# Queries and keys transposed in fp32 and split on the way out of PSUM, with a planner given new latencies, named buffers and a new order

## The chip, the cores and the metric

The kernel runs on one core of one Trainium2 chip. The core has a matrix engine (TensorE, "PE" in the profile, with its weight loads shown apart as "PEld"), a vector engine (DVE), a scalar engine (ACT), GpSimd (POOL), and a sync engine (SP) that issues the DMA transfers here. The on-chip memory is SBUF, 128 partitions wide; matrix results land in PSUM, which has 8 banks of 128 partitions by 512 fp32 values. The metric is the device time of one execution in microseconds (us); the number of a kernel is the median of its runs.

## The reference, cut to what matters

One inference step of four layers over 128 context tokens and 512 latent tokens, 1024 wide, with 16 query heads and 4 key/value heads of 64 values. Per layer and per group of tokens:

```python
u = rms_norm(h, norm_pre[l]) * (1 + scl) + shift          # scl, shift, gate from SiLU(cond) @ w_mod[l]
p = u @ w_in[l]                                           # 1024 x 2560
q, k, v, z = split(p, [1024, 1280, 1536])
q, k = rms_norm(q, q_norm[l]), rms_norm(k, k_norm[l])     # per head
# layers 0 and 3: rotary positions, all latent keys; layer 1: rotary, a band of +-128 keys and a sink logit;
# layer 2: a 2-D neighbourhood with a bias. Context keys are in every softmax of the latent tokens.
o = softmax(q @ k.T * 64 ** -0.5) @ v
h = h + gate * rms_norm((o * silu(z)) @ w_out[l], norm_post[l])
```

## The kernel before, in words

All data is fp32. A product that matters is made on PE from "fp32r" pieces: a value is rounded to a high part (fp32r) and what is left over is a low part, and PE sums high x high, high x low and low x high. The function `split` (L261, L262) makes the two parts of a 512-wide tile: ACT rounds (L261), DVE or POOL subtracts (L262).

The 640 tokens are five tiles of 128 (tile 0 is the context). Per layer the program does, in this order: `kv_chunk` (keys and values of all five tiles), and then twice, for chunk c = 0 and 1 of eight query heads, `q_chunk` (L597 ff.), the gates `z_block` (L634), the latent attention `lat_pair` four times, and the context attention `ctx_heads`; then `split_og` and `out_phase`, which ends with the normed and transposed input of the next layer.

The scores need the head's 64 values on the partitions. The queries' 128 partitions hold the high part of one head in 64 of them and the low part in the other 64, and the keys hold the same 64 values twice, once as a high tile and once as a low tile (`kst`, with room for two key heads, one buffer, so that chunk 1 builds it anew). Two matmuls of 128 partitions per score (L698, L724, L800) then give (q high + q low) x k high and (q high + q low) x k low.

Before, the parts are made ahead of the transpose. For each of the 40 query tiles (4 layers, 2 chunks, 5 token tiles) and each half of its eight heads, ACT rounds 128x256 values into a tile `hl` (L613), DVE or POOL subtracts (L615), PE transposes four 128x128 blocks with an fp32r identity (L620), and ACT or DVE copies the 128x512 PSUM bank to `q` (L256, a helper's line). For each of the 48 key tiles (4 layers, 2 chunks, 6 tiles, the cached one among them) `k_stack` does the same with the values doubled on the way: round (L544), subtract (L545), four transposes (L553), one copy of 512 columns (L256). The keys of heads 2 and 3 wait for chunk 1 in `kn2` (L591, "kn" in the profile).

The order on every engine is fixed when the program is built. `Sched.op` collects operations with the engines that may do each ("alts"), and `Sched.emit` places them one after another at the time that its own table of durations and latencies gives (`LAT` between engines, `TURN` between kinds of matmul, `SLACK`, and `DISLIKE` for a second choice of engine). `ORDER` shifts the priority of each part of the program ("ks" is `k_stack`, "qt" is `q_chunk`, "mf" the first modulation), and `WINDOW` says how many operations it may run ahead. A tile name is a tag with so many buffers: "B" is four one-bank PSUM buffers, through which every projection, transpose and attention output goes, and "S" is two two-bank ones for scores. The planner takes the buffer that it counts as free first; the tile framework hands out the buffers of a tag in turn.

Of the kernel before, what the change touches and what calls it, by code (L numbers as in the profile page):

```python
# [28 lines left out]
ORDER = {'hn': -470, 'up': -310, 'pv': 20, 'nat': 90, 'tab': -80, 'un': -170, 'bt': -280, 'st': -780, 'out': 230,  # L29
         'z': 90, 'og': -200, 'sc': 180, 'qt': -410, 'no': 180, 'ks': -170, 'mod': 160, 'w': -60}  # L30
MODSHIFT = 100
SSHIFT = -200
WINDOW = 520
PLAT = 270
XLAT = 180
SLACK = {'P': 140, 'V': 0, 'A': 220, 'G': 50, 'D': 80}
DISLIKE = {'Ap': 1060, 'mada': 3020, 'G1': 980, 'mad': 900, 'V': 1260, 'V2': 960, 'G': 780}
# [10 lines left out]
class Buf:  # L48


    def __init__(self, tag, shape, dt):
        self.tag, self.shape, self.dt = tag, shape, dt
        self.ap = None
        self.ops = 0
        self.freed = 0.0
        self.hist = []


class Sched:
# [3 lines left out]
    LAT = {("P", "P"): 0, ("V", "V"): 130, ("A", "A"): 155, ("G", "G"): 110, ("P", "V"): 200, ("P", "A"): 200,  # L63
           ("G", "V"): 80, ("A", "V"): 110, ("V", "A"): 135, ("G", "A"): 150, ("D", "D"): 100, ("V", "P"): 235, ("A", "P"): 228}
# [61 lines left out]
    def emit(self):  # L126
# [8 lines left out]
        slots = {t: [0.0] * c for t, (c, _) in self.tags.items()}  # L135
# [12 lines left out]
        while out < n:  # L148
# [3 lines left out]
            for e, lst in pend.items():  # L152
                cand = None
                for x in lst:
# [12 lines left out]
                    for b in self.ops[i][2]:  # L167
                        if b.ap is None:
                            m = need[b.tag] = need.get(b.tag, 0) + 1
                            s = slots[b.tag]  # L170
                            t = max(t, s[m - 1]) if len(s) >= m else 1e18
# [13 lines left out]
            for b in self.ops[i][2]:  # L185
                if b.ap is None:
                    slots[b.tag].pop(0)
# [7 lines left out]
            done[i] = t + dur + (2000 if e == "D" else 0)  # L195
            where[i] = e
            for b in self.ops[i][2]:
                b.ops -= 1
                b.freed = max(b.freed, done[i])
                if not b.ops:  # L200
                    bisect.insort(slots[b.tag], b.freed + (215 if b.tag in ("S", "B") else 150))
# [7 lines left out]
def build(ctx, tc, a, o):  # L209
# [5 lines left out]
    S = Sched(nc)  # L215

    def sbuf_tag(name, cap):
        S.tag(name, cap, lambda b: sb.tile(b.shape, b.dt, tag=name, name=name, bufs=cap))
# [320 lines left out]
    def k_stack(src, srckey, kst, ct, cap=None):  # L539

        hl = tmp([128, 2, 2, 2, 64], F32R)
        tc_ = [cap, kst] if cap else [kst]
        s = lambda: src()[:, :, None, :].to_broadcast([128, 2, 2, 64])
# [531 lines left out]
```

## Time and profile before

| | us |
|---|---|
| median of 3 runs | 1402.02 |
| lowest, highest | 1398.53, 1402.59 |
| the profiled execution, its own time | 1400.58 |
| its span, first to last instruction | 1398.5 |
| PE busy | 1357.7 |
| DVE busy | 954.7 |
| ACT busy | 758.6 |
| POOL busy | 266.8 |

PE's records are modelled at their ends: a matmul of 128 columns is shown as lasting 0.24 to 0.28 us while the next one starts 0.1 us later, so that PE's work is read from start to start, and a busy share near 100% is not PE at its peak. An idle time shown for PE is what is left after the modelled end of the last matmul.

### The profile page before, as it was taken

Reading aid. Unit: us, or ns where it says so; the run is one execution under the profiler, and the core shown is the slowest. Engines: PE = TensorE matmul, PEld = TensorE weight load, DVE = VectorE, ACT = ScalarE, POOL = GpSimd, SP = SyncE. Lnnn points to the kernel's source line nnn. Section 1 sums busy time; section 2 is a strip of 40 time slices with the busy share of each in tenths; the row PEclk is TensorE's granted clock in tenths of the full one; section 3 lists DMA queues with packets and bytes.
Section 4 is the critical chain, followed back from the end, with each engine's and each line's share of the span. In section 5 each row is a group of like instructions: output and inputs, shape, how many; then the busy total and the mean of one; then the engine's idle time right before and its main releaser. Section 6 shows DMA issues by size and latency. Waiting matters only on the chain.

```text
span 1398.5 us, 25496 instructions
## 1 busy us (share of the span) xinstructions
PE 1357.7 (97%) x9464; PEld 1122.3 (80%) x9464; DVE 954.7 (68%) x2300; ACT 758.6 (54%) x1854; POOL 266.8 (19%) x306
## 2 busy tenths in 40 slices
PE   6999999999999999999999999999999999999998
PEld 3788887888778887887878888888778888778876
DVE  4777667765587786777486676578488876577653
ACT  4556565554355565666354567468345555465641
POOL 1122012010032102201033541441033210021100
PEclk9999999999999999999999999999999999999999
DMA  8522222224532402324542522342633210111032
GB/s 305 175 69 84 61 91 84 69 87 140 181 115 67 147 30 91 125 92 161 161 125 73 157 57 91 98 141 85 196 126 101 91 53 10 61 52 41 31 123 103
DMA packets 73323, 145.11 MB, mean 104 GB/s; under 512 B 8752, under 2 KB 13936, under 8 KB 73200
## 3 DMA queue, kind: packets, MB, share of 16 engines
q1 hardware_dynamic: 73200, 143.50, 31.6%
q8 instruction: 74, 1.21, 0.4%
q14 instruction: 49, 0.40, 0.1%
HBM read 131.90 MB, written 11.57 MB: 103 GB/s over the span
## 4 chain that ended last, share of the span: by engine, by line
PE 83%; DVE 6%; ACT 4%; DMA 3%; issue 3%; POOL 0%; SPq 0%; DVEq 0%; POOLq 0%; ACTq 0%
PE B L497 21%; PE B L634 14%; PE B L780 8%; PE B L773 8%; PE S L901 8%; PE B L901 6%; PE S L698 5%; PE S L724 4%; PE B L383 3%; PE B L620 2%; PE S L497 1%; DVE w L262 1%; DMA raw<-in_w_mod 1%; DMA raw<-in_w_in 1%; PE B L451 1%
## 5 line engine op out<-in xcount | busy, mean ns | idle before, releaser
L307 POOL TENSOR_TENSOR sm<-sm,mhalf 128x1 f32<-128x1 f32 (+2 forms) x100 | 122.1, 1223 | 573.2 <-DVE sm L302 291.5
L497 PE MATMUL B<-w,uB 128*128 128x512 f32 x816 | 207.4, 401 | 0.0
L256 ACT ACTIVATE pt<-B 128x512 f32<-128x512 f32 (+1 forms) x228 | 126.9, 570 | 121.0 <-PE B L773 110.8
L497 PEld LDWEIGHTS B<-w,uB 128*128 128x128 f32 x816 | 149.2, 188 | 31.8 <-DVE uB L262 0.4
L634 PE MATMUL B<-uB,w 128*128 128x384 f32 x768 | 166.0, 348 | 0.6 <-DVE gate L642 0.3
L773 PE MATMUL B<-ident,p 128*128 128x128 f32 x1088 | 159.4, 276 | 3.1 <-ACT pt L256 2.3
L261 ACT ACTIVATE w<-raw 128x512 fp32r<-128x512 f32 x224 | 135.0, 627 | 30.2 <-PE B L901 8.0
L773 PEld LDWEIGHTS B<-ident,p 128*128 128x128 f32 x1088 | 125.1, 141 | 23.7 <-issue 13.6
L262 DVE TENSOR_TENSOR w<-raw,w 128x512 fp32r<-128x512 f32 x193 | 130.5, 700 | 13.0 <-ACT w L261 12.4
L497 PE MATMUL B<-w,uA 128*128 128x512 f32 x528 | 135.1, 403 | 1.1 <-DVE pt L256 0.8
L703 ACT ACTIVATE p<-S,sm 128x640 f32<-128x640 f32 x128 | 101.3, 794 | 59.6 <-DVE sm L701 54.6
L780 PE MATMUL B<-pt,vt 128*64 128x256 f32 (+1 forms) x1152 | 133.0, 376 | 0.0
L634 PEld LDWEIGHTS B<-uB,w 128*128 128x128 f32 x768 | 129.6, 188 | 3.7 <-issue 1.5
L701 DVE TENSOR_REDUCE sm<-S 128x1 f32<-128x640 f32 x128 | 102.7, 819 | 37.7 <-PE S L698 36.8
L634 PE MATMUL B<-uA,w 128*128 128x256 f32 x768 | 117.6, 290 | 0.3 <-DVE modc L394 0.3
L497 PEld LDWEIGHTS B<-w,uA 128*128 128x128 f32 x528 | 96.4, 188 | 24.7 <-DVE w L262 2.1
L780 PEld LDWEIGHTS B<-pt,vt 128*64 128x64 f32 x1152 | 77.5, 137 | 46.0 <-issue 11.4
L634 PEld LDWEIGHTS B<-uA,w 128*128 128x128 f32 x768 | 102.5, 189 | 3.4 <-issue 1.8
L658 DVE TENSOR_SCALAR p<-p,sm 128x640 f32<-128x640 f32 (+2 forms) x197 | 96.9, 506 | 6.6 <-DVE sm L657 0.5
L698 PE MATMUL S<-kst,q 128*128 128x320 f32 x512 | 96.8, 320 | 2.9 <-ACT p L703 2.8
L658 POOL TENSOR_SCALAR p<-p,sm 128x640 f32<-128x640 f32 (+2 forms) x59 | 44.0, 751 | 284.3 <-DVE sm L657 236.4
L737 ACT ACTIVATE p<-p,sm 128x512 f32<-128x512 f32 (+1 forms) x128 | 83.9, 657 | 6.4 <-DVE sm L735 6.3
(148 smaller groups left out, 2216.1 us busy)
## 6 DMA issues: line engine op xcount, KB each, us to landing
raw<-in_w_in SPq DMA_DIRECT2D x160, 256.0 KB
raw<-in_w_mod SPq DMA_DIRECT2D x160, 256.0 KB
raw<-in_w_out SPq DMA_DIRECT2D x64, 256.0 KB
w<-in_w_first SPq DMA_DIRECT2D x16, 512.0 KB
xs<-q SPq DMA_DIRECT2D x15, 512.0 KB
q<-xs SPq DMA_DIRECT2D x15, 512.0 KB
q<-in_x SPq DMA_DIRECT2D x10, 512.0 KB
kst<-gs SPq DMA_DIRECT2D x8, 512.0 KB
```

Of the source, the lines that this page charges most:

```text
L256: alts = {"A": Ap(n, lambda e: e.activation(out(), in_(), AF.Copy)), "V": V(n, lambda e: e.tensor_copy(out(), in_()))}
L261: S.op([As(n, lambda e: e.activation(h(), src(), AF.Copy))], r, w)
L262: f = lambda e: e.tensor_sub(l(), src(), h().bitcast(F32))
L307: S.op([("G", 395 + 157 * n, lambda e: e.tensor_tensor(r.ap, v.ap, mhalf.ap.to_broadcast([128, n]), op=OP.pow), "pow")], r=[v, mhalf], w=[r])
L497: e.matmul(ps(), t.ap[:, s, k, off:off + 128], W[k].ap[:, w], start=k == 0 and i == 0, stop=k == 7 and i == 2)
L634: e.matmul(ps.ap[:, 0:w], W[k].ap[:, wi, 128 * f:128 * f + 128], t.ap[:, s, k, :], start=k == 0 and i == 0, stop=k == 7 and i == 2)
L658: f = lambda e, i=i, p=p, w=w: e.tensor_scalar(p.ap[:, 0:w], p.ap[:, 0:w], rs.ap[:, i:i + 1], 1.0, op0=OP.mult, op1=OP.mult)
L698: e.matmul(ps.ap[:, b, 0:320], Q[t + 1].ap[:, hh], kst.ap[:, g, s, 320 * b:320 * b + 320], start=s == 0, stop=s == 1)
L701: S.op([V(640, lambda e, ps=ps, i=i: e.tensor_reduce(negm.ap[:, i:i + 1], ps.ap[:, :, 0:320], axis=AX.XY, op=OP.max, negate=True))], r=[ps ...
L773: e.transpose(pt.ap[:, c:c + 128], p.ap[:, b:b + 128], ident.ap)
L780: e.matmul(po.ap[64 * x:64 * x + 64, 256 * half + q0:256 * half + q0 + w], vt.ap[:, kt, 64 * g:64 * g + 64], sbt.ap[:, c0:c0 + w], start=f ...
L901: e.matmul(ps(), t.ap[:, s, k, off:off + 128], W[k].ap[:, w], start=k == 0 and i == 0, stop=k == 7 and i == 2)
```

## The change

The values are transposed first, in fp32, and split afterwards on the way out of PSUM.

Queries: per tile, PE transposes four 128x128 blocks of two heads each, in fp32 (L618 of the new file), into one PSUM bank. For each parity x of the head, ACT rounds the 64 partitions that hold those heads into `q` (64 x 512 values, L625), and DVE subtracts the rounded values from PSUM into the other 64 partitions of the same head (L626). The sum over the 128 partitions is the same; scores of a head wait for its parity and no longer for its half.

Keys: the doubling is a copy of its own (`kd`, ACT L595 or DVE L596; `kn2` is kept doubled, L592, and the cached keys are loaded twice by DMA). PE transposes two 128x128 blocks in fp32 (L550), ACT rounds 128x256 from PSUM into `kst` (L554), DVE subtracts into `kst` (L555).

Planner: other latencies, a landing time of 4 us for a DMA in place of 2, a `WINDOW` of 257 in place of 520, new weights, and a buffer of a tag is now a tag of its own ("B0" to "B3"), so that the buffer that the planner took is the one used.

```diff
-ORDER = {'hn': -470, 'up': -310, 'pv': 20, 'nat': 90, 'tab': -80, 'un': -170, 'bt': -280, 'st': -780, 'out': 230,
...
+ORDER = {'mf': -51, 'tab': 230, 'kv': 673, 'ks': -1156, 'nat': 29, 'hn': -564, 'mod': 211, 'w': -2, 'qt': 6,
...
-WINDOW = 520
...
+WINDOW = 257
 PLAT = 270
+LAND = 4000
...
-        slots = {t: [0.0] * c for t, (c, _) in self.tags.items()}
+        slots = {t: [(0.0, k) for k in range(c)] for t, (c, _) in self.tags.items()}
...
-                    slots[b.tag].pop(0)
+                    b.slot = slots[b.tag].pop(0)[1]
                     b.ap = self.tags[b.tag][1](b)
...
-        S.tag(name, cap, lambda b: pp.tile(b.shape, b.dt, tag=name, name=name, bufs=cap))
+        S.tag(name, cap, lambda b: pp.tile(b.shape, b.dt, tag="%s%d" % (name, b.slot), name=name, bufs=1))
...
-        hl = tmp([128, 2, 2, 2, 64], F32R)
...
-        S.op([As(256, lambda e: e.activation(hl.ap[:, 0], s(), AF.Copy))], r=[srckey], w=[(hl, 0)], touch=tc_)
-        f = lambda e: e.tensor_sub(hl.ap[:, 1], s(), hl.ap[:, 0].bitcast(F32))
-        S.op([G(256, f), VL(256, f)], r=[srckey, (hl, 0)], w=[(hl, 1)], touch=tc_)
...
+            for g in range(2):
+                e.transpose(ps.ap[:, 128 * g:128 * g + 128], src()[:, g].rearrange("p a d -> p (a d)"), ident.ap)
+        S.op([P(218, tr, "T")], r=[srckey, ident], w=[ps], touch=tc_)
+        v = lambda: ps.ap[:, 0:256].rearrange("p (g c) -> p g c", g=2)
+        d = lambda i: kst.ap[:, :, i, 128 * COL[ct]:128 * COL[ct] + 128]
+        S.op([As(256, lambda e: e.activation(d(0), v(), AF.Copy))], r=[ps], w=[(kst, ct)])
+        S.op([V(256, lambda e: e.tensor_sub(d(1), v(), d(0).bitcast(F32)))], r=[ps, (kst, ct)], w=[(kst, ct)])
...
+            pt = S.buf("B", [128, 512])
+
+            def tr(e, pt=pt, qn=qn):
+                for pr in range(4):
+                    e.transpose(pt.ap[:, 128 * pr:128 * pr + 128], qn.ap[:, 2 * pr:2 * pr + 2].rearrange("p h d -> p (h d)"),
+                                ident.ap)
+            S.op([P(436, tr, "T")], r=[qn, ident], w=[pt], touch=[cap])
+            for x in range(2):
+                hi, lo = (slice(0, 64), slice(64, 128))[::1 - 2 * x]
+                d = lambda rows, x=x, q=q: q.ap.rearrange("p (r x) t -> p x r t", x=2)[rows, x]
+                v = lambda hi=hi, pt=pt: pt.ap[hi].rearrange("p (r t) -> p r t", r=4)
+                S.op([As(512, lambda e, d=d, v=v, hi=hi: e.activation(d(hi), v(), AF.Copy))], r=[pt], w=[(q, x)], touch=[cap])
+                S.op([V(512, lambda e, d=d, v=v, hi=hi, lo=lo: e.tensor_sub(d(lo), v(), d(hi).bitcast(F32)))], r=[pt, (q, x)],
+                     w=[(q, x)], touch=[cap])
```

What the planner makes of it is seen in the instructions of each engine in program order. The rows give the line, the operation, the tiles out<-in, the shape written, and how many in a row.

PE in the projection of layer 0's first query chunk, before (L497 is the projection, L620 the query transposes, L698 scores):

```order
L497 MATMUL B<-w,uB 128x512 x21
L620 MATMUL B<-identr,tmp 128x128 x4
L497 MATMUL B<-w,uB 128x512 x3
L620 MATMUL B<-identr,tmp 128x128 x4
L497 MATMUL B<-w,uB 128x512 x18
L620 MATMUL B<-identr,tmp 128x128 x4
```

and now (L501 is the projection, L618 the query transposes, L387 a modulation):

```order
L618 MATMUL B<-ident,tmp 128x128 x4
L501 MATMUL B<-w,uA 128x512 x3
L501 MATMUL B<-w,uB 128x512 x30
L618 MATMUL B<-ident,tmp 128x128 x4
L501 MATMUL B<-w,uB 128x512 x18
L387 MATMUL B<-raw,cpad 32x128 x16
```

Where a query tile had two groups of four transposes, with projection matmuls between, it has one group of four.

PE at the change from chunk 0 to chunk 1 in layer 3, before (L800 context scores, L773 and L826 transposes of probabilities, L553 key transposes, L780 attention outputs, L634 gates):

```order
L634 MATMUL B<-uA,w 128x256 x9
L800 MATMUL S<-kst,q 128x128 x8
L773 MATMUL B<-ident,p 128x128 x8
L553 MATMUL B<-identr,tmp 128x128 x8
L780 MATMUL B<-pt,vt 64x256 x10
L553 MATMUL B<-identr,tmp 128x128 x16
L634 MATMUL B<-uB,w 128x384 x9
L826 MATMUL B<-ident,p 128x128 x4
```

and now (L804 context scores, L550 key transposes, which read `kn2` itself, L830 transposes of probabilities, L501 the projection of chunk 1):

```order
L638 MATMUL B<-uB,w 128x384 x24
L830 MATMUL B<-ident,p 128x128 x4
L804 MATMUL S<-kst,q 128x128 x8
L501 MATMUL B<-w,uA 128x512 x3
L550 MATMUL B<-ident,kn_11649 128x128 x6
L501 MATMUL B<-w,uA 128x512 x3
L550 MATMUL B<-ident,kn_11649 128x128 x2
L501 MATMUL B<-w,uA 128x512 x3
L550 MATMUL B<-ident,kn_11649 128x128 x4
```

The 24 key transposes became 12, and projection matmuls stand between their groups.

SP, the first transfers of the program, before (L340 and L344 load the first modulation weights, `cnd` is the conditioning vector, `q` the input rows):

```order
L280 DMA cnd<-in_cond 128x16
L329 DMA bcol<-in_vec 128x40
L296 DMA sink<-in_sink 128x16
L340 DMA w<-in_w_first 128x1024 x2
L969 DMA q<-in_x 128x1024
L340 DMA w<-in_w_first 128x1024 x2
```

and now:

```order
L344 DMA w<-in_w_first 128x1024 x4
L284 DMA cnd<-in_cond 128x16
L333 DMA bcol<-in_vec 128x40
L300 DMA sink<-in_sink 128x16
L973 DMA q<-in_x 128x1024
```

The conditioning vector now stands behind four transfers of 512 KB, and the first input rows behind the same four.

## Rows read from the trace of the kernel before

**Rows 1.** The page, busy time of each engine with its share of the span and its instructions, and TensorE's granted clock in 40 slices of the span (tenths of full speed).

```profile
PE 1357.7 (97%) x9464; PEld 1122.3 (80%) x9464; DVE 954.7 (68%) x2300; ACT 758.6 (54%) x1854; POOL 266.8 (19%) x306
...
PEclk9999999999999999999999999999999999999999
```

**Rows 2.** The page, the chain of work that ended last, shares of the span by engine.

```profile
PE 83%; DVE 6%; ACT 4%; DMA 3%; issue 3%; POOL 0%; SPq 0%; DVEq 0%; POOLq 0%; ACTq 0%
```

**Rows 3.** Busy time by stretch: the stretch and its length in us, busy us and instructions of each engine, granted clock, share of the DMA engines, GB/s. 400 to 457 and 1045 to 1110 are the starts of layers 1 and 3 (keys, values and queries).

```profile
0.00:50.00 50.00, 37.94 (x240) 24.15 (x240) 28.82 (x87) 21.20 (x53) 7.08 (x14) 1.00 0.85 302
...
400.00:457.00 57.00, 56.48 (x277) 45.57 (x277) 44.72 (x106) 30.05 (x68) 15.85 (x13) 1.00 0.24 78
...
1045.00:1110.00 65.00, 64.90 (x340) 53.95 (x339) 52.83 (x120) 36.80 (x82) 22.82 (x17) 1.00 0.24 80
1110.00:1200.00 90.00, 85.50 (x712) 71.42 (x711) 57.93 (x123) 52.38 (x126) 6.38 (x8) 0.98 0.14 47
...
1334.00:1398.50 64.50, 57.81 (x257) 45.56 (x255) 27.50 (x49) 16.62 (x40) 2.77 (x5) 0.97 0.32 111
```

**Rows 4.** PE in time order at the start of layer 1: start, length, engine, line, operation, out<-in, shapes, how many in a row.

```profile
405.29 4.39 PE L497 MATMUL B<-w,uB 128*128 128x512 f32 x18
...
409.51 0.46 PE L553 MATMUL B<-identr,tmp 128*128 128x128 f32 x4
...
409.81 0.93 PE L497 MATMUL B<-w,uB 128*128 128x512 f32 x3
...
410.58 0.46 PE L553 MATMUL B<-identr,tmp 128*128 128x128 f32 x4
...
410.88 3.74 PE L497 MATMUL B<-w,uB 128*128 128x512 f32 x15
```

**Rows 5.** PE in time order in layer 0, chunk 1, the same columns.

```profile
241.59 0.63 PE L634 MATMUL B<-uA,w 128*128 128x256 f32 x3
...
242.05 0.60 PE L773 MATMUL B<-ident,p 128*128 128x128 f32 x4
...
242.41 0.78 PE L634 MATMUL B<-uB,w 128*128 128x384 f32 x3
...
245.50 0.81 PE L620 MATMUL B<-identr,tmp 128*128 128x128 f32 x8
```

**Rows 6.** All engines in time order at the change of chunks in layer 3, the same columns as rows 4; in brackets the idle time before the piece and what ended it.

```profile
1189.13 1.07 PE L773 MATMUL B<-ident,p 128*128 128x128 f32 x8
...
1189.26 1.96 ACT L544 ACTIVATE tmp<-kn 128x256 fp32r<-128x256 f32 x6
...
1190.01 2.09 DVE L545 TENSOR_TENSOR tmp<-kn,tmp 128x256 fp32r<-128x256 f32 x6
...
1191.76 0.53 PE L553 MATMUL B<-identr,tmp 128*128 128x128 f32 x4 [1.56 <-ACT pt L256]
...
1193.05 3.76 PE L780 MATMUL B<-pt,vt 128*64 128x256 f32 x20
...
1196.74 1.05 PE L553 MATMUL B<-identr,tmp 128*128 128x128 f32 x8
1197.50 2.32 ACT L256 ACTIVATE kst<-B 128x512 fp32r<-128x512 f32 x4 [2.58 <-PE B L553]
...
1198.15 1.02 PE L553 MATMUL B<-identr,tmp 128*128 128x128 f32 x8 [0.36 <-ACT kst L256]
...
1199.38 1.85 PE L634 MATMUL B<-uB,w 128*128 128x384 f32 x9 [0.21 <-ACT kst L256]
```

**Rows 7.** What PE waited for: us in total, times, longest.

```profile
PE B L773 <- ACT pt L256: 2.3, 5, 0.7
...
PE B L553 <- ACT pt L256: 1.9, 2, 1.6
```

**Rows 8.** Groups by line, the copies, roundings and subtractions that stand nearest to the old and the new ones: busy us, mean ns of one | idle us before them, and what ended it.

```profile
L256 ACT ACTIVATE q<-B 128x512 fp32r<-128x512 f32 x78 | 45.0, 595 | 31.9 <-PE B L620 31.6
...
L615 DVE TENSOR_TENSOR tmp<-tmp 128x256 fp32r<-128x256 f32 x78 | 32.2, 435 | 12.9 <-ACT tmp L613 12.7
...
L613 ACT ACTIVATE tmp<-tmp 128x256 fp32r<-128x256 f32 x80 | 29.5, 410 | 68.1 <-DVE tmp L534 41.9 <-DVE tmp L528 26.0
...
L945 DVE TENSOR_TENSOR tmp<-B,kst 128x512 f32<-128x512 f32 x20 | 13.7, 687 | 21.0 <-ACT tmp L943 21.0
```

**Rows 9.** Groups by line, work that DVE and POOL share, and DVE's work on a query tile; columns as in rows 8.

```profile
L262 DVE TENSOR_TENSOR w<-raw,w 128x512 fp32r<-128x512 f32 x193 | 130.5, 700 | 13.0 <-ACT w L261 12.4
...
L658 DVE TENSOR_SCALAR p<-p,sm 128x640 f32<-128x640 f32 (+2 forms) x197 | 96.9, 506 | 6.6 <-DVE sm L657 0.5
...
L658 POOL TENSOR_SCALAR p<-p,sm 128x640 f32<-128x640 f32 (+2 forms) x59 | 44.0, 751 | 284.3 <-DVE sm L657 236.4 <-DVE sm L654 14.3 <-DMA raw<-in_w_in 13.3
L262 POOL TENSOR_TENSOR w<-raw,w 128x512 fp32r<-128x512 f32 x31 | 43.6, 1409 | 138.4 <-ACT w L261 135.8 <-issue 2.6
...
L510 DVE TENSOR_TENSOR tmp<-B,sm 128x512 f32<-128x512 f32 (+1 forms) x56 | 34.2, 611 | 44.4 <-POOL sm L307 44.3
...
L528 DVE TENSOR_TENSOR tmp<-tmp 128x512 f32<-128x512 f32 (+1 forms) x36 | 21.8, 606 | 0.3
```

**Rows 10.** DVE in time order at the start of layer 1, columns as in rows 4.

```profile
412.66 0.42 DVE L521 TENSOR_TENSOR tmp<-tmp,tab 128x256 f32<-128x256 f32 x1
...
413.00 0.42 DVE L523 TENSOR_TENSOR tmp<-tmp,tab 128x256 f32<-128x256 f32 x1
```

More of the change, by code (lines that the diff above doesn't have):

```diff
@@ L53, in __init__ @@
         self.ap = None
+        self.slot = 0
         self.ops = 0
@@ L170, in emit @@
                             s = slots[b.tag]
-                            t = max(t, s[m - 1]) if len(s) >= m else 1e18
+                            t = max(t, s[m - 1][0]) if len(s) >= m else 1e18
                     if t < 1e17:
@@ L194, in emit @@
                 last = x[2][3]
-            done[i] = t + dur + (2000 if e == "D" else 0)
+            done[i] = t + dur + (LAND if e == "D" else 0)
             where[i] = e
@@ L200, in emit @@
                 if not b.ops:
-                    bisect.insort(slots[b.tag], b.freed + (215 if b.tag in ("S", "B") else 150))
+                    bisect.insort(slots[b.tag], (b.freed + (170 if b.tag in ("S", "B") else 190), b.slot))
             out += 1
@@ L590, in kv_chunk @@
                 S.op([D(128, lambda e: e.dma_start(o["nv"][0, l].rearrange("t h d -> t (h d)"), vt.ap[:, VC, :]))], r=[(vt, VC)])
-            S.op([As(128, lambda e, kn=kn, ct=ct: e.activation(kn2.ap[:, ct], kn.ap[:, 2:4], AF.Copy))], r=[kn], w=[(kn2, ct)],
+            two = lambda k0, kn=kn: kn.ap[:, k0:k0 + 2, None, :].to_broadcast([128, 2, 2, 64])
+            S.op([As(256, lambda e, two=two, ct=ct: e.activation(kn2.ap[:, ct], two(2), AF.Copy))], r=[kn], w=[(kn2, ct)],
                  touch=[cap])
-            k_stack(lambda kn=kn: kn.ap[:, 0:2], kn, kst, ct, cap)
+            kd = tmp([128, 2, 2, 64])
+            S.op([As(256, lambda e, two=two, kd=kd: e.activation(kd.ap, two(0), AF.Copy)),
+                  V2(256, lambda e, two=two, kd=kd: e.tensor_copy(kd.ap, two(0)))], r=[kn], w=[kd], touch=[cap, kst])
+            k_stack(lambda kd=kd: kd.ap, kd, kst, ct, cap)
         return kst, vt, kn2
@@ L699, in mm @@
                                      start=s == 0, stop=s == 1)
-                S.op([P(588, mm)], r=[(Q[t + 1], hh // 4)] + [(kst, x) for x in range(5)], w=[ps], seq="s")
+                S.op([P(588, mm)], r=[(Q[t + 1], hh % 2)] + [(kst, x) for x in range(5)], w=[ps], seq="s")
                 S.op([V(640, lambda e, ps=ps, i=i: e.tensor_reduce(negm.ap[:, i:i + 1], ps.ap[:, :, 0:320], axis=AX.XY, op=OP.max,
@@ L724, in mm @@
                             e.matmul(ps.ap[:, i, o:o + n], Q[t + 1].ap[:, hh], v(s), start=s == 0, stop=s == 1)
-                S.op([P(w * 0.88 + 14, mm)], r=[(Q[t + 1], hh // 4)] + [(kst, x) for x in BAND[t]], w=[(ps, i)], seq="s")
+                S.op([P(w * 0.88 + 14, mm)], r=[(Q[t + 1], hh % 2)] + [(kst, x) for x in BAND[t]], w=[(ps, i)], seq="s")
                 bb, bap = bias[t]
```

52 lines of the change are left out of this document (17 added, 35 removed).

## Prediction

> **What bounds the kernel now.** I read the page's busy times first. PE is busy for 1357.7 of 1398.5 us at the full granted clock in every slice; DVE has 954.7 us and ACT 758.6 [rows 1]. The chain that ended last agrees: 83% of it is PE, 6% DVE, 4% ACT, 3% DMA [rows 2]. So a us of work taken from PE is a us of time, unless PE waits for data at that place, and work on DVE and ACT counts only where it makes PE wait. Then the stretches, for where PE stands idle: 40.8 us in all (1398.5 - 1357.7), of which 12.1 us lie in the first 50 us, where DMA runs at 302 GB/s, 6.7 us in the last 64.5, and 4.5 us between 1110 and 1200 [rows 3]. Some 17.5 us are left for all the rest. Last, the timeline, from start to start, for what a transpose costs PE.
>
> **PE's transposes.** Eighteen projection matmuls of 512 columns take 4.22 us to the next start, 0.234 each, so that a matmul of 256 columns is half, 0.117 [rows 4]. A group of four fp32r transposes takes 0.30 us from its first start to the next projection matmul (409.51 to 409.81, 410.58 to 410.88). The second of these begins 0.77 us after three projection matmuls that need 0.70, so 0.07 us late; with that the group costs 0.37 us [rows 4]. The fp32 transpose is there already, for the probabilities. Four of them begin 0.46 us after three matmuls that need 0.35, which is 0.11 late, and hold PE for 0.36 us, together 0.47 [rows 5]; eight in a row last 1.07 us against 0.60 for four, 0.12 each [rows 5, 6].
>
> A query tile has two groups of four before, 0.74 us, and one now, 0.47. Over 40 tiles that is 40 x 0.27 = 10.8 us. A key tile has one group of four before, 0.37, and two transposes now, 0.47 - 2 x 0.12 = 0.23; 48 x 0.14 = 6.7 us. Together -17.5 us, of which I take -17, since some groups stand back to back before and pay the 0.07 once (eight last 0.81 us against 0.46 for four [rows 4, 5]). If the late starts belong to the neighbours and not to fp32r, the group costs 0.30 and the saving is 40 x 0.13 + 48 x 0.07 = 8.6 us. If they belong to fp32r alone and the fp32 group costs 0.36, it is 40 x 0.38 + 48 x 0.25 = 27 us. I stay at 17, which charges both kinds alike.
>
> **The change of chunks.** In layer 3 the keys of chunk 1 are rounded by ACT (1.96 us for six), subtracted by DVE (2.09 us), transposed in 24 pieces and copied by ACT (four copies in 2.32 us), and the key buffer is single. PE starts its first group at 1191.76 after 1.56 us idle and reaches the gates at 1199.38, 7.62 us later; its work in between is 24 x 0.09 for the transposes (0.81 / 8 is 0.10 with the tail [rows 5]) and 20 x 0.117 for the attention output, 4.5 us [rows 6]. So PE loses 1.56 + 3.1 = 4.7 us there. Now the doubled keys lie ready in `kn2`, the first step is the transpose itself, and the list of PE shows three projection matmuls between the groups. What is late next are ACT's rounding and DVE's subtraction into `kst`, and their first readers are scores that come after the projection, so the projection hides them. I take -5 us for all four layers: layer 3 nearly whole, and little elsewhere. Bounds: nothing, if the same idle time returns ahead of the first transposes, and -9 if the other layers hold as much again.
>
> **Buffers and order.** PE waits for a "B" bank that ACT or DVE has still to empty: 2.3 us for the probabilities' transposes, 1.9 us for the keys' [rows 7], and smaller ones. A buffer used out of turn ends some of these, and the new order can end others. Apart from the first 50 us, the last 64.5 and the 4.7 us above, about 17 us of idle time are there to be had. I take -5, near what the bank waits sum to. It cannot be below -17; on the other side, a poor order could add as much as the start shows, +12.
>
> **The start.** `cnd`, which the first matmul needs, stands behind four transfers of 524 KB now and stood ahead of all. At 302 GB/s [rows 3] four take 6.9 us, and the first matmul needs two of them anyway, so it comes up to 3.5 us later. As the same bytes must land by about 50 us, most of it is made up again. I take +1, between -2 and +3.5.
>
> **ACT and DVE.** A query tile cost ACT 2 x (0.410 + 0.595) = 2.01 us and now two roundings of 64 x 512 from PSUM, which I price as the copy of the same 512 columns, 2 x 0.595 = 1.19 [rows 8]. It cost DVE 2 x 0.435 = 0.87, and now 2 x 0.687 = 1.37, by the nearest subtraction-like row with a PSUM input and 512 columns [rows 8]: half the lanes stand idle, so the values cost nearly twice. That is +0.50 x 40 = 20 us on DVE. The planner also gives DVE 47 of the 59 scalings that POOL did (47 x 0.506 = 24 us) and 19 of its 31 weight subtractions (19 x 0.70 = 13 us) [rows 9], and takes the copies of transposed probabilities from it (72 of 76 go to ACT), which about repays this. Price zero, hidden by PE; the price without that cover is the last rival.
>
> A subtraction that reads 64 partitions and writes the other 64 has no row before. Two DVE instructions of the usual kind overlap: one starts at 412.66, lasts 0.42 us, and the next starts at 413.00, 0.08 us before its end [rows 10]. [...]
>
> **The sum.** -17 - 5 - 5 + 1 = -26 us. The profiled execution took 1400.58 us, of which 2.1 us lie outside its span, and 1400.6 - 26 = 1374.6. The median of the runs is 1402.0, 1.4 us above the profiled one, and 0.1% is less than I can tell apart. I predict 1374 us, with 1366 to 1382 for this case by itself.
>
> **The rivals.** *Only the transposes.* The order and the buffers bring nothing and the idle time moves elsewhere: 1400.6 - 17 + 1 = 1384.6, and up to 1394 with the lower bound of the transposes. For it: the planner's table of durations is not the chip, and 17 us of idle time over 1300 us is already little. Against: the 4.7 us in layer 3 hang on a chain that the change takes apart.
>
> *The idle time goes.* The named buffers end the bank waits and the order most other idle time: -17 - 8 - 13 + 0, 1362.6 us. For it: PE is at 98% outside the first 50 us, so its waits are short and many, the kind that a better order ends. Against: many of them are latencies between engines that no order removes where nothing else is ready.
>
> *The saving is hidden.* PE waits for the last query tile anyway, and its shorter transposes only lengthen that wait: 1400 us. For it: ACT's rounding waited 41.9 + 26.0 us for the query tiles' last DVE step [rows 8], so that chain is late. Against: PE itself has only 0.5 us idle in 400 to 457 and 0.1 in 1045 to 1110 [rows 3], where these chains lie.
>
> *DVE becomes late, and the kernel slower.* The place is the projection of queries at the start of a layer. DVE is at 52.8 of 65 us from 1045 to 1110, 81% [rows 3]. A query tile costs DVE one reduction and one scaling of about 0.61, three rope steps of 0.606 and the subtractions 0.87, 3.9 us, and 8 x 0.70 / 5 = 1.1 us of weight subtractions go with it [rows 8, 9], 5.0 in all; PE needs 24 x 0.234 = 5.6 us for the tile [rows 4]. With 0.50 more and POOL's share of the weights, DVE stands at 5.5 to 6, and it decides from 5.6 on. At 6.3 us, with other work between, each of 40 tiles loses 0.7, 28 us: 1400.6 - 17 + 1 + 28 = 1413 us. [...] Against: PE has key transposes, modulations and gates to put in between.
>
> **How the numbers follow.** The forecast has 0.50, only the transposes 0.22, the idle time goes 0.16, the saving is hidden 0.05, DVE late 0.07. A difference under 0.3% (4.2 us) I call no change, about what a measurement of this kernel can tell. Faster: 0.50 + 0.22 + 0.16 = 0.88; same 0.05; slower 0.07. The range runs from 1357, just under the case in which the idle time goes, to 1394, the worst of only the transposes; what is outside is the two last cases and the tails, under 0.2.
>
> **What would show it.** 160 transposes on L618 and 96 on L550, with groups of four at 0.36 to 0.47 us from start to start. At the change of chunks in layer 3 no wait of PE ahead of the key transposes. L625 near 0.6 us, L626 near 0.7. PE's idle time between the first 50 us and the last 64 at about 12 us. PE at its first matmul some 3 us later than before. I am wrong if PE's idle time grows in 400 to 457 or 1045 to 1110 behind L626 or L555 (DVE late), or if PE's transposes do not get cheaper by the count.

## The result, and the profile after

| | before | after |
|---|---|---|
| median of the runs, us | 1400.28 (4 runs) | 1367.61 (4 runs) |
| lowest, highest | 1398.34, 1402.59 | 1366.54, 1369.06 |
| profiled execution, own time and span | 1400.58, 1398.5 | 1366.54, 1364.8 |

The ratio is 0.9767, interval 0.9745 to 0.9788: 32.7 us less, where 26 were forecast. The time lies in the forecast's own range and the direction is right. The runs below show that its parts were not: with the new planner the data path brought half of what was forecast for it, and the planner four times as much.

The page of after, busy times and the chain by engine; they answer to [rows 1, 2].

```profile
PE 1331.3 (98%) x9208; PEld 1097.1 (80%) x9208; DVE 971.9 (71%) x2298; ACT 753.5 (55%) x1823; POOL 212.9 (16%) x231
...
PE 80%; DVE 13%; issue 3%; ACT 2%; POOL 1%; DMA 1%; SPq 0%; DVEq 0%; POOLq 0%; ACTq 0%
```

Of the 33.7 us by which the span fell (1398.5 - 1364.8), 26.4 are PE's busy time (1357.7 - 1331.3) and 7.3 its idle time (40.8 - 33.5). DVE is 17.2 us busier and POOL 53.9 us less.

Busy time by stretch, columns as in [rows 3]: the start, the start of layer 1, the middle, the change of chunks in layer 3, the end.

```profile
0.00:50.00 50.00, 37.57 (x267) 24.43 (x268) 31.11 (x97) 23.01 (x58) 6.72 (x13) 1.00 0.88 314
...
400.00:457.00 57.00, 55.74 (x327) 45.34 (x326) 45.82 (x102) 25.18 (x50) 15.62 (x11) 1.00 0.31 100
50.00:1300.00 1250.00, 1235.74 (x8683) 1026.66 (x8682) 912.63 (x2153) 712.48 (x1723) 203.46 (x213) 1.00 0.31 98
1110.00:1200.00 90.00, 89.44 (x655) 75.24 (x654) 58.81 (x118) 53.58 (x127) 4.76 (x4) 1.00 0.14 47
1300.00:1364.80 64.80, 58.04 (x262) 46.02 (x260) 28.15 (x51) 18.02 (x43) 2.76 (x5) 0.96 0.34 118
```

Idle time of PE (a stretch less PE's busy time in it): 12.4 us at the start (12.1 before), 14.3 in the middle (22.0 before, which is 40.8 - 12.1 - 6.7), 6.8 at the end (6.7). All of the gain in idle time lies in the middle. In 1110 to 1200 it is 0.6 us, against 4.5 [rows 3].

The timeline of the start of layer 1, columns as in [rows 4, 6]: one query tile.

```profile
425.09 2.35 PE L501 MATMUL B<-w,uA 128*128 128x512 f32 x9
...
427.28 0.60 PE L618 MATMUL B<-ident,tmp 128*128 128x128 f32 x4
...
427.63 1.65 PE L501 MATMUL B<-w,uA 128*128 128x512 f32 x6
427.91 1.20 ACT L625 ACTIVATE q<-B 64x512 fp32r<-64x512 f32 x2 [4.05 <-PE B L618]
...
429.14 1.39 DVE L626 TENSOR_TENSOR q<-B,q 64x512 fp32r<-64x512 f32 x2 [2.59 <-ACT q L625]
```

Nine projection matmuls need 9 x 0.234 = 2.11 us, the transposes begin 2.19 us after the first of them, 0.08 late, and hold PE for 0.35: 0.43 for the group, read as the prediction reads it. The single starts in the trace show that this lateness does not stand ahead of the transposes. It is in the second matmul behind a group, which comes 0.30 us (fp32r, before) or 0.32 us (fp32, now) after the first in place of 0.23. The bank that they fill is free again at 430.53, when DVE's second subtraction ends, 2.9 us after PE has left it. Remember this span; the experiments come back to it.

Over all 40 query tiles the bank is held for a median 2.92 us behind the transposes; before, one copy emptied it, in a median 0.80 us (80 groups). The four steps that empty it now go one after another: in 37 of the 40 tiles the first subtraction starts only when the second rounding has ended, 0.64 us or more after the first rounding, which is the only one that it reads. That wait is part of the 2.9 us; no run takes it away.

The change of chunks in layer 3, the same columns, in place of [rows 6].

```profile
1176.62 0.92 PE L501 MATMUL B<-w,uA 128*128 128x512 f32 x3
...
1177.37 0.81 PE L550 MATMUL B<-ident,kn 128*128 128x128 f32 x6
1177.79 0.94 ACT L554 ACTIVATE kst<-B 128x256 fp32r<-128x256 f32 x3 [1.22 <-PE B L550]
...
1177.94 0.96 PE L501 MATMUL B<-w,uA 128*128 128x512 f32 x3
1178.20 1.08 DVE L555 TENSOR_TENSOR kst<-B,kst 128x256 fp32r<-128x256 f32 x3 [0.19 <-ACT kst L554]
...
1178.74 0.38 PE L550 MATMUL B<-ident,kn 128*128 128x128 f32 x2
...
1178.88 0.95 PE L501 MATMUL B<-w,uA 128*128 128x512 f32 x3
```

No PE row has a bracket, so the trace shows no wait of PE here: the projection matmuls fill the time in which ACT and DVE empty the banks.

Groups by line, columns as in [rows 8].

```profile
L626 DVE TENSOR_TENSOR q<-B,q 64x512 fp32r<-64x512 f32 x80 | 55.1, 689 | 34.9 <-ACT q L625 33.8
...
L625 ACT ACTIVATE q<-B 64x512 fp32r<-64x512 f32 x80 | 47.4, 593 | 54.4 <-PE B L618 53.7
...
L618 PE MATMUL B<-ident,tmp 128*128 128x128 f32 x160 | 24.8, 277 | 6.1 <-DVE tmp L532 5.1 <-DVE tmp L538 0.6 <-DVE modc L398 0.3
...
L550 PE MATMUL B<-ident,tmp 128*128 128x128 f32 x48 | 9.1, 273 | 0.0
...
L550 PE MATMUL B<-ident,kn 128*128 128x128 f32 x48 | 7.2, 273 | 0.0
```

The counts are those forecast: 160 transposes on L618 and 96 on L550.

PE's waits: us in total, times, longest.

```profile
PE B L350 <- DMA raw<-in_w_in: 10.9, 1, 10.9
PE B L618 <- DVE tmp L532: 5.1, 10, 0.7
...
PE B L777 <- ACT pt L260: 0.8, 3, 0.5
```

The largest wait behind the start is now that for the last rope step of a query tile (L532), ten times half a microsecond; the wait of the probabilities' transposes for a bank fell from 2.3 us [rows 7] to 0.8, and that of the key transposes is gone.

### The profile page after: what moved, and what is told of

The parts are those of the page before. It is cut to its first block, busy times and chain, and to the rows that moved or that the text cites. A ratio compares the mean times of both kernels' runs of the same rounds, so it can differ in the third digit from the quotient of the medians.

```text
span 1364.8 us, 24827 instructions
## 1 busy us (share of the span) xinstructions
PE 1331.3 (98%) x9208; PEld 1097.1 (80%) x9208; DVE 971.9 (71%) x2298; ACT 753.5 (55%) x1823; POOL 212.9 (16%) x231
## 4 chain that ended last, share of the span: by engine, by line
PE 80%; DVE 13%; issue 3%; ACT 2%; POOL 1%; DMA 1%; SPq 0%; DVEq 0%; POOLq 0%; ACTq 0%
PE B L501 16%; PE B L638 13%; PE B L777 9%; PE B L784 9%; PE S L905 8%; PE B L905 6%; PE S L702 5%; PE S L728 4%; PE B L387 2%; DVE q L626 2%; DVE tmp L467 1%; POOL sm L311 1%; DVE w L266 1%; PE S L501 1%; PE B L618 1%
## 5 line engine op out<-in xcount | busy, mean ns | idle before, releaser
L311 POOL TENSOR_TENSOR sm<-sm,mhalf 128x1 f32<-128x1 f32 (+2 forms) x100 | 130.3, 1305 | 667.6 <-DVE sm L306 352.5
L260 ACT ACTIVATE pt<-B 128x512 f32<-128x512 f32 (+1 forms) x300 | 161.2, 575 | 101.8 <-PE B L777 91.7
L501 PE MATMUL B<-w,uB 128*128 128x512 f32 x816 | 201.3, 399 | 0.0
L501 PEld LDWEIGHTS B<-w,uB 128*128 128x128 f32 x816 | 150.0, 188 | 33.4 <-issue 0.2
L777 PE MATMUL B<-ident,p 128*128 128x128 f32 x1088 | 155.1, 277 | 2.1 <-ACT pt L260 0.8
L266 DVE TENSOR_TENSOR w<-raw,w 128x512 fp32r<-128x512 f32 x212 | 141.7, 698 | 5.7 <-ACT w L265 5.2
L777 PEld LDWEIGHTS B<-ident,p 128*128 128x128 f32 x1088 | 122.5, 140 | 24.0 <-issue 8.8
L501 PE MATMUL B<-w,uA 128*128 128x512 f32 x528 | 136.9, 403 | 0.8 <-DVE tmp L467 0.7
L265 ACT ACTIVATE w<-raw 128x512 fp32r<-128x512 f32 x224 | 131.7, 626 | 6.6 <-PE B L638 2.8
L662 DVE TENSOR_SCALAR p<-p,sm 128x640 f32<-128x640 f32 (+2 forms) x244 | 123.7, 519 | 6.8
L638 PE MATMUL B<-uA,w 128*128 128x256 f32 x768 | 114.7, 286 | 0.1
L501 PEld LDWEIGHTS B<-w,uA 128*128 128x128 f32 x528 | 95.1, 188 | 23.0 <-issue 2.6
L702 PE MATMUL S<-kst,q 128*128 128x320 f32 x512 | 100.5, 324 | 1.1 <-ACT p L707 0.8
L510 ACT ACTIVATE tmp<-B 128x512 f32<-128x512 f32 (+1 forms) x56 | 30.1, 537 | 106.0 <-PE B L501 82.6
```

The source lines that it names most:

```text
L260: alts = {"A": Ap(n, lambda e: e.activation(out(), in_(), AF.Copy)), "V": V(n, lambda e: e.tensor_copy(out(), in_()))}
L265: S.op([As(n, lambda e: e.activation(h(), src(), AF.Copy))], r, w)
L266: f = lambda e: e.tensor_sub(l(), src(), h().bitcast(F32))
L311: S.op([("G", 395 + 157 * n, lambda e: e.tensor_tensor(r.ap, v.ap, mhalf.ap.to_broadcast([128, n]), op=OP.pow), "pow")], r=[v, mhalf], w=[r])
L501: e.matmul(ps(), t.ap[:, s, k, off:off + 128], W[k].ap[:, w], start=k == 0 and i == 0, stop=k == 7 and i == 2)
L638: e.matmul(ps.ap[:, 0:w], W[k].ap[:, wi, 128 * f:128 * f + 128], t.ap[:, s, k, :], start=k == 0 and i == 0, stop=k == 7 and i == 2)
```

## The experiments

The change has three parts: the data path (transpose, then split), the buffers by name, and the planner's numbers. Two theories stood against each other. By the first the terms add: each part brings its own share whatever the others are. By the second the data path alone gives little or loses, because the bank is held while ACT and DVE split, and only an order made for that brings the gain out. Every kernel below computes the whole reference. The number given first is the median, the one in brackets the ratio to the kernel before, run on the same chip, with its interval; that kernel's medians there were 1398.7 to 1399.8 us.

### The data path alone: slower

```diff
 # before, with k_stack, kv_chunk, q_chunk of after
 WINDOW = 520
+LAND = 2000
 # ORDER, LAT, SLACK, DISLIKE and the buffers in turn as before
```

> The transposes in fp32 and the split from PSUM alone; latencies, weights, window and buffers in turn as before. Theory A (the parts add: some 18 us of PE work from the transposes and some 15 us of waits from the planner): 1382 us, 1377 to 1387, PE idle about as before, 41 us. Theory B (the gain is the search's, and PE's saved work turns into waits without it): 1393 us or more, PE idle 50 us or more.

Measured: 1410.83 us (1.0097, 1.0071 to 1.0122), 12 us slower than before. What PE waited for:

```profile
PE B L616 <- DVE tmp L530: 4.4, 8, 0.8
PE B L636 <- DVE q L624: 3.9, 3, 1.3
PE B L548 <- DVE kst L553: 3.7, 6, 1.6
...
PE B L548 <- DMA tmp<-in_cache_k: 2.7, 4, 1.2
```

The second and third lines are new waits: gates (L636) and key transposes (L548) wait for a bank which DVE's subtractions from PSUM (L624, L553) still read. The last is new too: the cached keys are transposed as they land, and four times PE waits for their transfer. Neither before nor after has such a wait. The timeline of PE at the change of chunks in layer 2:

```profile
863.67 0.38 PE L548 MATMUL B<-ident,kn 128*128 128x128 f32 x2
865.63 0.44 PE L548 MATMUL B<-ident,kn 128*128 128x128 f32 x2 [1.58 <-DVE kst L553]
867.00 0.60 PE L548 MATMUL B<-ident,kn 128*128 128x128 f32 x2 [0.93 <-DVE kst L553]
868.25 0.66 PE L548 MATMUL B<-ident,kn 128*128 128x128 f32 x2 [0.65 <-DVE tmp L512]
868.71 1.06 PE L775 MATMUL B<-ident,p 128*128 128x128 f32 x4
```

And the stretches there, columns as in [rows 3]:

```profile
860.00:866.00 6.00, 4.42 (x22) 3.23 (x21) 2.72 (x7) 2.93 (x12) 0.27 (x1) 1.00 0.31 106
866.00:872.00 6.00, 3.94 (x16) 2.69 (x15) 2.88 (x6) 2.74 (x6) 1.38 (x1) 0.59 0.00 0
872.00:878.00 6.00, 5.11 (x24) 3.10 (x25) 1.72 (x4) 1.28 (x3) 0.00 (x0) 0.55 0.00 0
```

With the old order the key transposes follow each other with nothing between, and PE does eight of them in 5 us. The first two waits are for a bank that L553 reads; the third is for one that holds a projection of queries, until its norm has read it (L512). Behind that, the granted clock is lower: 0.59 and 0.55 of full speed in the two stretches from 866 to 878 us, against 1.00 ahead of them. The mean is 0.57 over 12 us, by which I estimate a loss of up to 12 x 0.43 = 5 us of PE's work. In all PE is idle for 55.2 us of 1407.8, 14.4 more than before. Its busy time fell by only 5.1 us (1357.7 to 1352.6), although it has 256 matmuls less to do.

### The planner and the names on the old data path

```diff
 # before, with ORDER, shifts, WINDOW, LAND, LAT, SLACK, DISLIKE and the named buffers of after
```

> The planner's part alone (latencies, landing time, weights, window, named buffers) on the old way of splitting ahead of the transpose. Theory A: 1386 us, 1381 to 1392, PE idle about 30 us. Theory B: 1378 us or less. Theory C (weights searched for one program are worth nothing on another): 1397 us or more.

Measured: 1379.00 us (0.9858, 0.9838 to 0.9877). The new numbers bring 20 us without any change of the data path. Together with the run before: -20 and +12 would add to -8; the change brings -31 to -33. The terms do not add, so the second theory stands in its main point, though the time is a microsecond above the 1378 that it allowed.

This run also prices the data path where it is used. It and after have the same planner and the same names, and their tiles lie alike (the step of their matmuls, explained below, is 232.2 ns in both). Its page:

```profile
PE 1348.1 (98%) x9464; PEld 1119.5 (81%) x9464; DVE 941.5 (68%) x2286; ACT 789.2 (57%) x1935; POOL 215.6 (16%) x239
```

Against after (1331.3) the new path takes 16.8 us from PE's busy time. PE's idle time is 4.5 us longer with it (33.5 against 1377.1 - 1348.1 = 29.0), and the median falls by 10.6 us (1379.0 to 1368.4). So the same path is worth -11 us with the new planner and +12 with the old one.

And it shows where the wait at the change of chunks in layer 3 went, for here the keys are still split ahead of the transpose:

```profile
1190.60 1.14 PE L557 MATMUL B<-identr,tmp 128*128 128x128 f32 x12
1191.58 0.94 PE L501 MATMUL B<-w,uA 128*128 128x512 f32 x3
1192.35 1.14 PE L557 MATMUL B<-identr,tmp 128*128 128x128 f32 x12
```

All 24 old key transposes (L557) stand between projection matmuls, and no row has a bracket: the new order alone ends that wait.

### The names alone

```diff
-        S.tag(name, cap, lambda b: sb.tile(b.shape, b.dt, tag=name, name=name, bufs=cap))
+        S.tag(name, cap, lambda b: sb.tile(b.shape, b.dt, tag="%s%d" % (name, b.slot), name=name, bufs=1))
 # the same for PSUM; all else as before
```

> Named buffers alone on the kernel before. Theory A, as in the prediction: -5 us, 1395 us, PE's waits for a bank on L773, L553 and L620 (5.6 us before) mostly gone. Rival: the buffers in turn were the planner's choice nearly always, 1400 us, the same waits.

Measured: 1393.42 us (0.9962, 0.9949 to 0.9974), 5.4 us less, which is the size forecast. But not for the reason given. Its waits for banks are those of [rows 7] to the digit:

```profile
PE B L774 <- ACT pt L257: 2.3, 5, 0.7
PE B L554 <- ACT pt L257: 1.9, 2, 1.6
```

No wait for a bank went, so the gain came from elsewhere. The trace has one thing more, at the change of chunks in layer 3. After the same wait of 1.55 us the 20 attention outputs take

```profile
1189.15 2.38 PE L781 MATMUL B<-pt,vt 128*64 128x256 f32 x20
```

where before they took 3.76 [rows 6]. The granted clock is 1.00 here; in the profiled execution of before it stood at 0.50 from 1194 to 1197 us, columns as in [rows 3]:

```profile
1194.00:1197.00 3.00, 3.00 (x16) 1.46 (x13) 0.87 (x2) 0.92 (x6) 0.00 (x0) 0.50 0.00 0
```

### After, with the buffers in turn

```diff
-        S.tag(name, cap, lambda b: sb.tile(b.shape, b.dt, tag="%s%d" % (name, b.slot), name=name, bufs=1))
+        S.tag(name, cap, lambda b: sb.tile(b.shape, b.dt, tag=name, name=name, bufs=cap))
 # the same for PSUM; all else as after
```

> The changed kernel with its buffers handed out in turn again, the order of the instructions unchanged. Theory A: 1373 us, 1370 to 1377, waits for banks come back. Rival: 1367 to 1369 us, names are worth nothing.

Measured: 1363.05 us (0.9749, 0.973 to 0.9768): 5 us faster than after, where 5 slower were expected, or no difference. The order of the instructions is the same in both. What differs is where the tiles lie in SBUF, and it shows in how long the same matmuls take: the last 96 of the program (w_out, 512 columns) in the chain of waits, columns start, length, piece, of after

```profile
1330.12 22.33 PE B L905 x96
```

and of this kernel

```profile
1326.23 21.99 PE B L905 x96
```

They wait for nothing inside, and take 3.5 ns less each (0.34 us / 96). No run had changed the place alone yet; the next one does.

### Moving the tiles by 32 bytes

```diff
 # the kernel with the buffers in turn
-    keps = persist("keps", [128, 1])
+    keps = persist("keps", [128, 9])
```

One constant is 32 bytes longer, so that what is allocated behind it, `uA` and `uB` among it, begins 32 bytes later. Nothing else changes.

> The changed kernel with its buffers in turn, every instruction the same and in the same order, but one constant made 32 bytes longer, so that the inputs' tiles uA and uB and all behind them lie 32 bytes further in SBUF, while the weights' tiles stay. Theory H (names and turns differ by where the tiles lie: the 2400 projection matmuls of 512 columns started 229.3 ns apart there and 232 to 234 ns apart in the other kernels, whose tiles lie otherwise): steps of 232 to 234 ns, 6 to 10 us more than with the buffers in turn, 1369 to 1373 us. Rival (what differs are the waits for buffers): 1362 to 1365 us, steps of 229 ns.

Measured: 1369.34 us (0.9798, 0.9775 to 0.9822), 6.3 us slower than without the 32 bytes. The same piece of the chain:

```profile
1331.53 22.41 PE B L905 x96
```

With 32 bytes moved and nothing else, the time thus grew by 6.3 us. From the start times of the 2400 projection and output matmuls of 512 columns, the mean step from one to the next, by where the operands in the weights tile `w` and the input tile `u` begin in SBUF (bytes in the partition, remainder by 64; the addresses are those of the built programs, the steps are from the traces):

| kernel | w, u | step, ns |
|---|---|---|
| before; the data path alone, and with 'pv' (below) | 0, 32 | 234.0 |
| after, mean 232.2 | mixed: 1080 of 2400 at 32, 0, 720 at 32, 32 | by place 231.1 to 233.0 |
| after, buffers in turn; the data path with the new ORDER (below) | 32, 32 | 229.3 |
| the same, 32 bytes moved | 32, 0 | 233.1 |

The remainder by 64 alone does not tell the step: at 32, 32 it is 229.3 ns with the buffers in turn and 231.1 in after. By the steps the 32 bytes would cost 2400 x 3.8 ns = 9.1 us, of which 6.3 came out in the time; presumably some of these matmuls do not bound it. From before to after the mean falls by some 1.8 ns, and up to 2400 x 1.8 = 4.3 us of the result may be placement, which nobody set. Of the names' 5.4 us this may be a part as well (step 234.0 to 232.8, up to 2400 x 1.2 = 2.9 us). Both are estimates from the steps. At the start that kernel is 2.4 us ahead of before at the same matmul (at 46 us) and keeps 1.4 of it from 52 us on. The rest of the 5.4 is not told apart.

### After with the old weights

```diff
 # after, with ORDER, shifts, WINDOW, LAND, SLACK, DISLIKE of before
 # (LAT and the named buffers stay new)
```

> The changed kernel with the new latencies and named buffers, but the old weights, window, slack and landing time. Theory D (the weights found by the search carry the gain: without them PE waits behind the split of the keys at the change of chunks): 1395 to 1412 us, idle time of PE ahead of the key transposes in layers 2 and 3 as in the run of the data path alone. Rival (the latencies, and the names, carry it): 1380 us or less.

Measured: 1403.74 us (1.0028, 1.001 to 1.0045). The weights carry the gain: 35 us lie between this kernel and after (1368.39 beside it), and by the step of its matmuls (232.8 against 232.2 ns) I put up to 2400 x 0.6 = 1.4 of them down to placement. The place of its waits is not quite the one expected: the key transposes wait 1.3 us in all for a bank that the subtraction reads, against 3.7 in the data path alone, but scores wait 5.3 us for the queries' subtraction itself (L625 of this kernel), and the query transposes 5.2 us for the rope step.

### Only the queries new, old planner

```diff
 # before, with the query half of the data path (L613 to L626); keys as before
```

> Only the queries on the new way, keys on the old one, planner as before. Theory D (what cost the data path alone its 12 us is the key split, whose banks are held through ACT and DVE): 1386 to 1392 us, near the 10.8 us that the query transposes take from PE. Rival (the query split costs as much, by DVE's longer subtraction): 1398 us or more.

Measured: 1404.49 us (1.0036, 1.0021 to 1.005), 5 us slower than before. The idea that the keys alone cost the 12 us fell: the queries cost 5 of them, and the keys add about 7. The wait for the rope step and the one for the queries' bank are as with both halves:

```profile
PE B L616 <- DVE tmp L530: 5.0, 9, 0.8
PE B L636 <- DVE q L624: 3.8, 3, 1.3
```

### The weights rounded, and after again

```diff
-ORDER = {'mf': -51, 'tab': 230, 'kv': 673, 'ks': -1156, 'nat': 29, 'hn': -564, ...
+ORDER = {'mf': -50, 'tab': 230, 'kv': 670, 'ks': -1160, 'nat': 30, 'hn': -560, ...
-WINDOW = 257
+WINDOW = 260
```

> The changed kernel with each weight rounded to tens and a window of 260 in place of 257, a neighbour of the order found. If the search found one lucky order, a neighbour loses most of the planner's share: 1376 us or more. If the weights stand for a rule (keys early, the softmax early), the neighbour is within 4 us: 1363 to 1372.

> The changed kernel again, beside the others on one chip: 1365 to 1370 us. If it lies at 1363 here, the buffers in turn gained nothing over the names in the earlier run.

Measured: 1369.98 us (0.9788, 0.9756 to 0.9819) and 1368.39 us (0.9772, 0.9745 to 0.98). The gain does not hang on the exact numbers: it outlives the rounding of the weights. The step is a small one, though. No weight moves by more than 5, and PE has the same instruction at 8314 of its 9208 places, so a farther neighbour might still lose the gain.

### The data path with the new ORDER alone, and with one entry of it

```diff
 # the data path alone, with the whole ORDER of after
```

> The data path with the planner as before and only the table of the parts' weights from the change: latencies, window, slack, dislikes, shifts and landing time as before, buffers in turn. Theory J (that table is what turns the loss of the data path into the gain): 1375 to 1387 us. Rival (it needs the other numbers with it): 1395 us or more.

Measured: 1384.74 us (0.9908, 0.9882 to 0.9934), 26 us less than the data path alone. But this kernel is no clean comparison, for its tiles came to lie at 32, 32, where the step is 229.3 ns, and those of the data path alone at 0, 32. By the steps that is 2400 x 4.7 = 11 us, and some 8 if as much of it comes out as with the 32 bytes (6.3 / 9.1). So the priorities themselves have about 15 to 18 of the 26, an estimate from the steps; they were not run at the old placement.

```diff
 # the data path alone
-ORDER = {'hn': -470, 'up': -310, 'pv': 20, ...
+ORDER = {'hn': -470, 'up': -310, 'pv': -1242, ...
```

> As the data path alone, with one weight changed: the part that transposes probabilities and makes the attention outputs gets -1242 in place of 20, so that it goes as soon as it can and projections are left to stand between the waits. Theory K (this one weight is half of it): 1390 to 1400 us. Rival: 1406 us or more, since at the change of chunks in layers 0, 2 and 3 no projection stands between the key transposes with it.

Measured: 1400.11 us (1.0005, 0.9988 to 1.0022), 11 us less than the data path alone, at the edge of what was expected. This comparison is clean: the step is 234.0 in both. 'pv', the attention outputs and the transposes of probabilities before them, is less than half of the 26 but most of the 15 to 18 that belong to the order. It brings the path level with before, no more.

### The fastest order with the start of before

```diff
 # after, buffers in turn; the tiles kept at the same remainders by padding
+    S.shift = -3000    # cnd is loaded ahead of the weights
```

> The changed kernel with its buffers in turn and the conditioning vector loaded first, the tiles placed as with the buffers in turn modulo 128 bytes. Theory I (PE's first matmul waits for the vector, 10.5 us in place of 6.5, and the start is made up only in part): first matmul at 6 to 7 us, 1359 to 1361 us. Rival (the start is bound by the bytes of the transfers): 1362 to 1364 us.

Measured: 1362.98 us (0.9756, 0.9733 to 0.9779), no different from the 1363.05 without it. PE's first wait:

```profile
PE B L352 <- DMA w<-in_w_first: 5.5, 1, 5.5
```

The first matmul comes 5.0 us earlier (10.5 there), and by 77 us PE has done 63.55 us of work against 63.52. So the start is not bound by when the first matmul comes. That it is bound by the bytes that must land fits the DMA engines' busy share of 0.86 and 0.89 in the first 50 us of the two kernels, but was not tested by itself.

## Why the prediction was right and wrong

**PE's transposes, -17.** The sizes were right. With the longer step behind it counted in, a group of four old transposes between projection matmuls costs PE a median 0.37 us (43 groups in before; 0.37 was forecast), four new ones 0.44 (24 groups in after; 0.47), two new ones 0.22 (22 groups; 0.23). By these the saving is 40 x 0.30 + 48 x 0.15 = 19 us, and the run with the new planner on the old path has 16.8 us more PE busy time than after. What failed is taking the term for itself, with "DVE late" and "the saving is hidden" as the only ways to lose it: of 16.8 us of PE's work 11 came out as time with the new order, and with the old order the new path is 12 us slower. A bank used to be released by one copy; now it is held through two roundings and two subtractions (0.80 and 2.92 us), and there are four such banks for all of PE's work. The rival that ended on the slower side had the direction of that, but the wrong resource: DVE is at 80% in 400 to 457 (45.82 / 57; 78% before), so it has time to spare, and the waits point to its place behind ACT in the holding of a bank. That is read from the waits; no run changed the holding time, or the number of banks, alone.

**The change of chunks, -5.** In after it is as forecast: the wait ahead of the key transposes is gone. But the sentence on what is late next, that rounding and subtraction go into `kst` and only scores wait for them, was wrong by itself. In the data path alone the next key transposes wait 1.58 and 0.93 us for a bank that the subtraction still reads. The projection matmuls between the groups hide that. They do the same for the old key transposes (L557 in the run with the old path and the new planner), so the -5 belongs to the order and not to the shorter chain. The 4.7 us that the term was read from were not all waits either: the kernel with the names alone has the same waits there and the clock at 1.00, and its 20 attention outputs take 2.38 us in place of 3.76. So some 1.4 us of the 4.7 stood beside a granted clock of 0.50 in that one execution, which the prediction, with "the full granted clock in every slice", did not see; [rows 3] shows 0.98 in that stretch.

**Buffers and order, -5.** The term that failed most, in size and in cause. The bank waits of [rows 7] were to go through the names; the names alone left them as they were, and the kernel with buffers in turn is the faster one. What the names can be seen to do is to move tiles in SBUF. The order, for which next to nothing was forecast, with the planner's other numbers, is worth 14 us on the old data path (1379.0 against 1393.4, both with names, the latencies among the numbers, 1.4 of it placement by the steps) and 35 on the new one (1403.7 against 1368.4, both with names and the new latencies). I had measured it by PE's idle time before, 17 us in the middle; but its worth on the new path is in waits that the old trace could not show, since they did not exist there.

**The steps from before to after**, in the order of the runs: the data path +12 (1410.8); ORDER -26 (1384.7), of which 8 to 11 are placement by the estimate above; the planner's other numbers, with buffers still in turn and at the same placement, -22 (1363.05); the names +5 (1368.4), which by the steps is placement given back (229.3 to 232.2 ns). Together -31. Taken the other way round, the planner with its names is -20 on the old path, and the path then -11. The forecast had -5 for the first and -17 - 5 = -22 for the second. So the sum came near because a data path that took too much for granted, by 11 us, and an order priced too low, by 15, erred in opposite directions: a right total from wrong parts, which is luck. By the size of the planner's share the rival in which the idle time goes (-8 - 13) was the nearer one, and its 1362.6 us are 5.0 from the 1367.6 measured, the forecast's 1374 are 6.4.

**The start, +1.** Right, and shown: PE's first matmul is 4.5 us later (10.9 against 6.45), its idle time in the first 50 us grew by 0.4, and moving `cnd` back to the front brings nothing (1362.98 against 1363.05). The term itself is nearer to 0 than to 1.

**ACT and DVE, 0.** Right. L625 takes 593 ns and L626 689, as priced (595 and 687), DVE is 17.2 us busier, and PE has 1.3 us idle in 400 to 457 against 0.5, the waits for the last rope step (L532), not for L626. The two subtractions of a tile take 1.39 us in the timeline, 2 x 0.69, so they don't overlap. Over the whole trace of after the next DVE instruction, where it follows without a wait, starts a median 81 ns before its predecessor ends; into a L626 it starts 14 ns after the end (49 pairs), behind one 31 ns after it (73 pairs). That is about 0.1 us per neighbour (81 + 14 and 81 + 31 ns). The two counts share the 30 pairs in which one L626 follows another, so some 92 starts lose their overlap, by my estimate about 9 us of DVE time. What holds these starts back is not shown. The price of zero held: in after PE waits for L626 twice, 0.5 us each time (ahead of L728 and L777).

**PE idle in the middle, about 12 us.** 14.3.

**What stays open.** Why the step of a matmul changes with where its tiles lie: the runs show 229.3 against 233.1 ns for 32 bytes, and no more. Which of latencies, window, slack, dislikes, landing time and shifts make the 22 us was not separated, and neither were the entries of ORDER beside 'pv'. How ORDER's 26 us divide between priorities and placement is estimated and not run. Other placements were not tried. That the longer hold of the banks is what turns the path's gain into a loss under the old order is read from waits. Why the first subtraction of a tile waits for the second rounding, and what the 0.6 us would bring, was not tested. In the data path alone PE's busy time is 21 us above after's; by the estimates above the slower clock has up to 5 of it and placement up to 4.3; the rest is stalls that the modelled ends show as busy, which I infer and did not measure.

## What to carry to other kernels

Price a change of data path by how long each shared buffer is held as well as by the work it removes, and ask what stands between two users of that buffer in the order: the same path cost 12 us with the old planner's numbers (1410.8 against 1398.8) and gained 11 with the new ones (1368.4 against 1379.0), each time with the tiles lying alike. A wait that does not exist in the old trace cannot be read there, so test the path with the old order and the order with the old path before adding terms; a total that comes out right does not show that its terms were. Two kernels with different allocation are not compared until the same long matmul piece has been read in both traces, since 32 bytes of shift moved this one by 6.3 us.

## What was not expected of the hardware

The mean step of the 512-column matmuls on rounded fp32 was 229.3 ns at one placement of their operands in SBUF and 233.1 with the inputs 32 bytes further on, with the same instructions in the same order; the second kernel took 6.3 us more than the first one's 1363. In before, with another order and a third placement, the step was 234.0.

In the data path alone PE's granted clock was 0.59 and 0.55 in the 12 us behind eight transposes spread over 5 us, with waits between them, and 1.00 again from 878 us. The clock behind a wait is not always the same: behind one of 1.56 us in layer 3 it was 0.50 for 3 us in the profiled execution of before, and behind the same wait 1.00 in that of the kernel with the names alone. In after the same stretch is filled with projection matmuls, and the granted clock in the middle is 1.00.
